# Placing accumulating transfers in the second token half, and contiguous FFN weights, in a gated-linear-attention encoder block

## The chip, the cores and the metric

The kernel runs on one core of a Trainium2 chip. The metric is the device time of one execution in microseconds (us). A core has a matrix engine (TensorE, "PE" in the profile, with its weight loads as "PEld"), a vector engine (VectorE, "DVE"), a scalar engine (ScalarE, "ACT"), a general one (GpSimd, "POOL") and SyncE ("SP"), which here only issues transfers. Each engine works through its own queue in a fixed order. DMA transfers are issued from the queues of SP, ACT and POOL; an instruction or an issue that must wait holds up everything behind it in its queue.

## The reference

One layer on 2048 tokens of width 1024, all in float32: a chunked gated linear attention mixer, then a feed-forward network with a causal convolution, each with a residual, and a final norm.

```python
h = rmsnorm(x, mix_norm_w)
x = x + gla_mixer(h, w_in, w_gate2, b_gate, norm_w, w_out)   # 4 heads, chunks of 64
h = rmsnorm(x, ffn_norm_w)
u = causal_dwconv(h @ w_up, conv_w, conv_b)   # 1024 -> 2 x 2816, 3 taps along the tokens
g, val = jnp.split(u, 2, axis=-1)
x = x + (jax.nn.silu(g) * val) @ w_down       # 2816 -> 1024
return rmsnorm(x, final_norm_w)
```

## The kernel before

**Products.** Large products are done in a fast scheme of seven instead of eight block products (`p1` to `p7`, a 2 x 2 block scheme with sums of blocks as operands). Each operand is split into a rounded part and a remainder (`split`, lines 188 and 189: a cast on ACT, a subtraction on DVE), and each block product is three matmuls per 128-wide slice (`mm3p`, lines 179 to 181).

**Stages.** The mixer's passes run to about 850 us. Then comes the up phase (`phase_u`), then the down phase. The up phase takes the tokens in two halves, `s = 0` and `s = 1`, of 1024 tokens. In each half it runs over 11 groups `g`; a group is two feature tiles `f`, each with a gate part and a value part, and 14 jobs (seven products for two tiles), each job 12 matmuls. The profile names its accumulators `ua`, `ub` (product p2) and `uc`.

**Weights of a group.** `load(sg, n)` fetches the four weight blocks of a feature tile into two raw tiles `ur`, two blocks each, one transfer per block (line 1204). `prep`, five jobs ahead, adds and subtracts blocks on POOL (`us` and `ur`: lines 1214, 1217, 1220, 1232) and splits the result on ACT and DVE into `uw_p`.

**Accumulators.** Products p1, p6, p7 and p4 of one tile go on in one accumulator. After p1 and after p6 ACT copies it out (`copied`, line 1237, named `c`), and the next product may start only then. The results go into a tile `u` with two halo columns in front (`new_u`; POOL copies them, line 1243), of which three exist. `conv` does the taps on ACT (line 1253) and DVE (line 1255), `gated` the product of gate and value (line 1262).

**Operands of the down phase.** `gated` stores the seven token operands of the down product to the scratch `ad` in DRAM. In the second half four of them are sums that POOL makes (tiles `as`, line 1284). In the first half only blocks and parts are stored (line 1267), and the sums are made in DRAM: `gather` (line 1363) issues from POOL's queue a transfer that adds one stored operand onto another. There are four per group, each needing the one before it or the stores: p7 += p5, then p5 += p4, then p6 += p5, then p3 += p6. In the program they are written in the second half, at jobs 2, 5, 10 and 13 of a group, for the same or the preceding group of the first half (the last two in the down phase):

```python
GATHER = {2: ("p7", "p5", 0), 5: ("p6", "p5", 1), 10: ("p5", "p4", 0), 13: ("p3", "p6", 1)}
```

**Order.** The framework's planner, not the program's text, sets the order on each queue: among instructions whose inputs are ready in its model, it takes the earliest written one, and an engine that is free in the model takes a later one. No edge tied the gathers to the second half.

**Change of halves.** The seven operands of the hidden state for the new half (`h_p`, line 904, four transfers each) replace those of the old half one after another, as the last group of the first half is done with them; SP issues them, as it does the weight loads and the stores to `ad`.

**Conv weights.** `vectors` loads three taps and the bias as rows, transposes them on PE and copies them into `cw` (lines 603 to 611).

Of the kernel before, what the change touches and what calls it, by code (L numbers as in the profile page):

```python
# [10 lines left out]
F32 = mybir.dt.float32  # L11
# [3 lines left out]
ALU = mybir.AluOpType  # L15

P = 128
# [8 lines left out]
def hybrid_kernel(  # L26
# [10 lines left out]
    w_out: bass.AP,  # L37
    w_up: bass.AP,
    conv_w: bass.AP,
    conv_b: bass.AP,  # L40
    w_down: bass.AP,
    out: bass.AP,
):
    nc = tc.nc
    x = x[0]
    out = out[0]
    w_in, w_gate2, gla_norm_w, w_out = w_in[0], w_gate2[0], gla_norm_w[0], w_out[0]
    w_up, conv_w, conv_b, w_down = w_up[0], conv_w[0], conv_b[0], w_down[0]

    S, D = x.shape  # L50
    F = w_down.shape[0]
# [7 lines left out]
    HK = KT // 2  # L59
    NF = F // P  # L60
# [7 lines left out]
    SB = 8  # L68
# [43 lines left out]
    def scratch(shape, name):  # L112
        return dr.tile(shape, F32, tag=name, name=name)
# [10 lines left out]
    ad = {(s, o, q): scratch([P, 512], f"ad_{s}_{o}_{q}") for s in range(NS) for o in OPS for q in range(NQ)}  # L124

    def mm_ps(name):
        return ps.tile([P, 512], F32, tag="mm", name=name, bufs=4)

    def aux_ps(name):
        return ps.tile([P, 512], F32, tag="aux", name=name, bufs=4)  # L130

    def raw_tile(shape, name):
        return wr.tile(shape, F32, tag="raw", name=name, bufs=RB)
# [17 lines left out]
    def later_do(us, fn):  # L151
        heapq.heappush(delayed, (clock["now"] + us, next(seq), fn))
# [39 lines left out]
    ident = cst.tile([P, P], F32, name="ident")  # L192
# [3 lines left out]
    cw = cst.tile([P, 4, 2 * NF], F32, name="cw")  # L196
    halo = cst.tile([P, 2 * NF, 2], F32, name="halo")
# [161 lines left out]
    rows = {}  # L359
# [9 lines left out]
    rp = {}  # L369
# [187 lines left out]
    def gates(b, t0, t1, t2):  # L557
# [27 lines left out]
        def sums(tt):  # L585
            pd = aux_ps(f"pd_{b}_{tt}")
            for i in range(2):
                nc.tensor.matmul(pd, rp["later"], L[tt][1 - i], start=(i == 0), stop=(i == 1))
            nc.scalar.activation(es[tt], pd, AF.Exp, scale=-ITAU)
            t = b * NT + tt  # L590
            nc.sync.dma_start(ed[t], es[tt])
            later_do(TB3, lambda: totals(t, es[tt]))
            if tt + 1 < NT:
                later_do(0.4 * t2, lambda: halves(tt + 1))
# [3 lines left out]
        later_do(t0 + 4.0, lambda: halves(0))  # L598
        for tt in range(NT):
            later_do(t0 + t1 + t2 * tt, lambda tt=tt: sums(tt))  # L600


    def vectors():
        rws = rp["p"].tile([P, 512], F32, tag="s2k", name="rows", bufs=SB)
        for k in range(3):
            nc.sync.dma_start(rws[:2 * NF, k * P:(k + 1) * P], conv_w[k].rearrange("(f p) -> f p", p=P))
        nc.sync.dma_start(rws[:2 * NF, 3 * P:4 * P], conv_b.rearrange("(f p) -> f p", p=P))
        pt = aux_ps("pt_c")
        for k in range(4):
            nc.tensor.transpose(pt[:, k * 2 * NF:(k + 1) * 2 * NF], rws[:2 * NF, k * P:(k + 1) * P], ident[:2 * NF, :2 * NF])  # L610
        nc.vector.tensor_copy(cw.rearrange("p a b -> p (a b)"), pt[:, :8 * NF])


    sp = {}
# [567 lines left out]
    def tiles2(ap):  # L1182

        v = ap.rearrange("p (j c k) -> p c j k", c=2, k=P)
        return v[:, 0], v[:, 1]
# [1 line left out]
    def tiles1(ap):  # L1187
        return ap.rearrange("p (j k) -> p j k", k=P)

    wuv = w_up.rearrange("(kt p) c -> p kt c", p=P)  # L1190

    def phase_u():
        raws, wops, sums, made = {}, {}, {}, {}
        jobs = [(s, g, o, f) for s in range(NS) for g in range(NQ) for o in OPS for f in (2 * g, 2 * g + 1)]
# [3 lines left out]
        def load(sg, n):  # L1198
            s, g = divmod(sg, NQ)
            for f in (2 * g, 2 * g + 1):  # L1200
                r = raw_tile([P, 2, 512], f"ur_{s}_{f}_{n}")
                for i, (c, k) in enumerate((((f, 0), (NF + f, 0)), ((NF + f, 1), (f, 1)))[n]):
                    q = nc.scalar if s == 0 and g == 0 else nc.sync
                    q.dma_start(r[:, i, :].rearrange("p (k c) -> p k c", c=P), wuv[:, HK * k:HK * (k + 1), c * P:(c + 1) * P])
                raws[f, n] = r

        def prep(k):
# [32 lines left out]
        def new_u(s, i, f):  # L1240
            c = f + i * NF
            u = pools["us"].tile([P, TS + 2], F32, tag="u", name=f"u_{s}_{c}", bufs=3)
            nc.gpsimd.tensor_copy(u[:, 0:2], halo[:, c, :])
            made["u", i, f] = u
            return tiles2(u[:, 2:2 + TS])

# [41 lines left out]
        GATHER = {2: ("p7", "p5", 0), 5: ("p6", "p5", 1), 10: ("p5", "p4", 0), 13: ("p3", "p6", 1)}  # L1288

        load(0, 0)  # L1290
        load(0, 1)
        yield
        done = 0
        bank = {}
        for k, (s, g, o, f) in enumerate(jobs):
            if s == 1 and k % GJ in GATHER:
                dst, src, back = GATHER[k % GJ]
                gather(dst, src, g - back)
            if k % GJ in (2, 7) and k // GJ + 1 < NS * NQ:
                load(k // GJ + 1, int(k % GJ == 7))  # L1300
# [21 lines left out]
            if o == "p1":  # L1322
                a = bank["a", f] = mm_ps(f"ua_{s}_{f}")
                mm3p(a, pairs)
                made["p1", f] = copied(f"c1_{s}_{f}", a)
            elif o == "p5":
                c = bank["c", f] = aux_ps(f"uc_{s}_{f}")
                mm3p(c, pairs)
            elif o == "p6":
                a = bank["a", f]  # L1330
                mm3p(a, pairs, first=False, more=True)
                made["u2", f] = copied(f"c2_{s}_{f}", a)
            elif o == "p2":
                pb = mm_ps(f"ub_{s}_{f}")
                mm3p(pb, pairs)
                ev, _ = new_u(s, 0, f)
                nc.vector.tensor_add(ev, tiles1(pb), tiles1(made.pop(("p1", f))))  # L1337
            elif o == "p7":
                a = bank["a", f]
                mm3p(a, pairs, first=False, more=True)  # L1340
                u3 = pools["us"].tile([P, 512], F32, tag="as", name=f"c3_{s}_{f}", bufs=AB)
                nc.scalar.copy(u3, a)
                ev, od = new_u(s, 1, f)
                made["ev", f] = ev
                nc.vector.tensor_add(od, tiles1(bank["c", f]), tiles1(u3))
            elif o == "p4":
                a = bank.pop(("a", f))
                mm3p(a, pairs, first=False, more=True)
                nc.scalar.copy(made.pop(("ev", f)), tiles1(a))
                conv(s, 1, f)  # L1350
            else:
                c = bank.pop(("c", f))
                mm3p(c, pairs, first=False, more=True)
                _, od = tiles2(made["u", 0, f][:, 2:2 + TS])
                nc.vector.tensor_add(od, tiles1(c), tiles1(made.pop(("u2", f))))  # L1355
                conv(s, 0, f)
                gated(s, f)


    def gather(o, src, q):  # L1360

        if 0 <= q < NQ:
            nc.gpsimd.dma_start(ad[0, o, q], ad[0, src, q], accum_op=ALU.add, max_dma_last_dim=2048)

    units = [(o, s) for o in ("p1", "p5", "p6", "p7", "p2", "p4", "p3") for s in range(NS)]
    steps = [(o, s, q) for o, s in units for q in range(NQ)]
# [94 lines left out]
    xin[1] = load_x(1, "x")  # L1461
    first_pair()
    nc.scalar.dma_start(nw2, ffn_norm_w[0].rearrange("(kt p) -> p kt", p=P))
    later_do(12.0, vectors)
    for ps_ in PS:
        for j in range(int(ps_ == "R"), NP):
            unit(ps_, j)
# [62 lines left out]
    for n, (o, s) in enumerate(units):  # L1530
# [10 lines left out]
        for q in range(NQ):  # L1541
            k = n * NQ + q
# [18 lines left out]
_INS = [  # L1561
    "x", "mix_norm_w", "ffn_norm_w", "final_norm_w",
    "gla_w_in", "gla_w_gate2", "gla_b_gate", "gla_norm_w", "gla_w_out",
    "ffn_w_up", "ffn_conv_w", "ffn_conv_b", "ffn_w_down",
]
_OUTS = [((1, 2048, 1024), "float32")]

# [22 lines left out]
```

## Time and profile before

| | us |
|---|---|
| runs: median of 3 (lowest, highest) | 2170.98 (2165.34, 2174.02) |
| the profiled execution | 2172.34 |
| its span, first to last instruction | 2170.3 |
| PE busy | 2080.6 (96%) |
| DVE busy | 1627.6 (75%) |
| ACT busy | 1105.6 (51%) |
| POOL busy | 688.3 (32%) |

Busy shares are means over stages with different limits, so the stages are read one by one. "a<-b" in a row means that the instruction writes a and reads b; numbers at the end of tile names are left out. Rows of a view of waits give the waiting engine and line, what ended the wait, the us in total, how often, and the longest. Rows of a timeline give start, duration, engine, line, operation and, in brackets, the idle time of the engine just before and what ended it. "SPq", "ACTq" and "POOLq" are the queues' own instructions, among them the issues of transfers; "to landing" is the time from a transfer's issue to its data being there.

### The profile page before, as it was taken

How to read it: one execution, taken by the hardware profiler on the slowest of the kernel's cores; microseconds unless marked ns; L12 is line 12 of the kernel's file. 1: busy time of each engine (PE TensorE's matmuls, PEld its weight loads, DVE VectorE, ACT ScalarE, POOL GpSimd, SP SyncE). 2: the span in 40 equal slices, each digit the busy share in tenths (PEclk: the TensorE clock that was granted, in tenths of full speed). 3: DMA queues.
4: the chain of work that ended last, by engine and by line, in shares of the span. 5: the costliest groups of instructions: out<-in, count | busy, mean ns of one | idle time of the engine just before them, and what ended most of it. 6: DMA issues, size and time to landing. Idle time of an engine off the chain costs nothing.

```text
span 2170.3 us, 28933 instructions
## 1 busy us (share of the span) xinstructions
PE 2080.6 (96%) x9832; PEld 1723.4 (79%) x9832; DVE 1627.6 (75%) x2168; ACT 1105.6 (51%) x2024; POOL 688.3 (32%) x606
## 2 busy tenths in 40 slices
PE   6999999989998998899999997999999999999998
PEld 5888788878887877688787786888888877888886
DVE  8756888799888664678988875988788777457564
ACT  5555755665565775454554543554445533233342
POOL 2000011111111002345446444665665444036010
PEclk9999999999999999999999999999999999999999
DMA  6646684578557899686676679342424567354453
GB/s 220 224 165 212 211 296 139 157 228 300 170 190 261 315 332 363 224 220 157 174 199 155 177 198 294 97 122 83 136 73 122 185 244 281 95 184 160 142 180 115
DMA packets 328357, 423.30 MB, mean 195 GB/s; under 512 B 24446, under 2 KB 183342, under 8 KB 328208
## 3 DMA queue, kind: packets, MB, share of 16 engines
q1 hardware_dynamic: 284336, 346.99, 48.8%
q10 hardware_dynamic: 37536, 62.93, 8.6%
q0 software_dynamic: 6336, 11.54, 3.5%
q8 instruction: 77, 1.26, 0.2%
q14 instruction: 72, 0.59, 0.1%
HBM read 278.23 MB, written 154.66 MB: 199 GB/s over the span
## 4 chain that ended last, share of the span: by engine, by line
PE 56%; DMA 14%; DVE 13%; issue 7%; POOL 4%; ACT 3%; SPq 2%; ACTq 0%; DVEq 0%; POOLq 0%
PE pd_p L180 5%; PE pd_p L181 5%; PE pd_p L179 5%; PE ua L179 4%; PE ua L181 4%; PE ua L180 4%; DVE t L1255 3%; DMA ad_p<-ad_p 3%; PE uc L179 2%; PE uc L181 2%; PE uc L180 2%; PE mp_R L179 2%; PE mp_R L181 2%; PE mp_R L180 2%; PE mp_A L181 1%
## 5 line engine op out<-in xcount | busy, mean ns | idle before, releaser
L179 PE MATMUL ua<-h_p,uw_p 128*128 128x512 f32 x704 | 278.6, 396 | 23.9 <-ACT c L1237 23.9
L1255 DVE SCALAR_TENSOR_TENSOR t<-u,cw,t 128x1024 f32<-128x1024 f32 x176 | 285.3, 1625 | 11.9 <-ACT t L1253 10.9
L180 PE MATMUL ua<-h_p,uw_p 128*128 128x512 f32 x704 | 276.4, 393 | 0.0
L181 PE MATMUL ua<-h_p,uw_p 128*128 128x512 f32 x704 | 276.3, 392 | 0.0
L180 PE MATMUL pd_p<-dw_p,da 128*128 128x512 f32 x616 | 240.3, 390 | 3.4 <-DVE da L189 3.4
L179 PE MATMUL pd_p<-dw_p,da 128*128 128x512 f32 x616 | 240.1, 390 | 0.6 <-DVE u L1337 0.6
L181 PE MATMUL pd_p<-dw_p,da 128*128 128x512 f32 x616 | 240.0, 390 | 0.0
L189 DVE TENSOR_TENSOR da<-da_p,da 128x512 fp32r<-128x512 f32 x154 | 133.7, 921 | 104.5 <-ACT da L188 104.4
L188 ACT CAST da<-da_p 128x512 fp32r<-128x512 f32 x154 | 85.3, 619 | 207.2 <-PE pd_p L181 147.2
L188 ACT CAST uw_p<-us 128x512 fp32r<-128x512 f32 x132 | 82.1, 622 | 203.9 <-POOL us L1217 124.3
L179 PEld LDWEIGHTS ua<-h_p,uw_p 128*128 128x128 f32 x704 | 133.5, 190 | 58.6 <-ACT c L1237 31.5
L189 DVE TENSOR_TENSOR uw_p<-us,uw_p 128x512 fp32r<-128x512 f32 x132 | 136.3, 1038 | 51.7 <-ACT uw_p L188 50.4
L189 DVE TENSOR_TENSOR uw_p<-ur,uw_p 128x512 fp32r<-128x512 f32 x176 | 143.2, 842 | 40.8 <-ACT uw_p L188 40.6
L181 PEld LDWEIGHTS ua<-h_p,uw_p 128*128 128x128 f32 x704 | 133.4, 190 | 28.2
L180 PEld LDWEIGHTS ua<-h_p,uw_p 128*128 128x128 f32 x704 | 133.6, 190 | 27.4
L179 PE MATMUL uc<-h_p,uw_p 128*128 128x512 f32 x352 | 138.1, 392 | 4.5 <-issue 4.5
L1253 ACT ACTIVATE t<-u,cw 128x1024 f32<-128x1024 f32 x88 | 109.7, 1247 | 60.9 <-DVE u L1355 53.0
L180 PE MATMUL uc<-h_p,uw_p 128*128 128x512 f32 x352 | 137.8, 392 | 0.7 <-DVE uw_p L189 0.7
L180 PEld LDWEIGHTS pd_p<-dw_p,da 128*128 128x128 f32 x616 | 115.7, 188 | 28.6 <-DVE da L189 4.7
L181 PE MATMUL uc<-h_p,uw_p 128*128 128x512 f32 x352 | 137.6, 391 | 0.0
L179 PEld LDWEIGHTS pd_p<-dw_p,da 128*128 128x128 f32 x616 | 115.7, 188 | 25.1 <-DVE u L1337 1.0
L181 PEld LDWEIGHTS pd_p<-dw_p,da 128*128 128x128 f32 x616 | 115.7, 188 | 23.8
(278 smaller groups left out, 5340.9 us busy)
## 6 DMA issues: line engine op xcount, KB each, us to landing
ur<-in_ffn_w_up_dram SPq DMA_DIRECT2D x168, 256.0 KB, 4.0
da_p<-ad_p SPq DMA_DIRECT2D x154, 256.0 KB, 4.0
h_p<-hd_p SPq DMA_DIRECT2D x56, 512.0 KB, 8.6
ad_p<-t SPq DMA_DIRECT2D x110, 256.0 KB, 3.2
x<-in_x_dram SPq DMA_DIRECT2D x32, 512.0 KB, 4.7
ch<-in_ffn_w_down_dram SPq DMA_DIRECT2D x61, 256.0 KB, 3.7
hr_A_p<-h1d_p SPq DMA_DIRECT2D x56, 256.0 KB, 2.9
hr_B_p<-h1d_p SPq DMA_DIRECT2D x56, 256.0 KB, 3.3
```

The costliest lines, as they stand in the source:

```text
L179: nc.tensor.matmul(ps_ap, ah, bl, start=(first and i == 0), stop=False, **kw)
L180: nc.tensor.matmul(ps_ap, al, bh, start=False, stop=False, **kw)
L181: nc.tensor.matmul(ps_ap, ah, bh, start=False, stop=(last and i == len(pairs) - 1), **kw)
L188: nc.scalar.copy(hi, src)
L189: nc.vector.tensor_sub(lo, src, f32(hi))
L1253: nc.scalar.activation(t, u[:, 2:2 + TS], AF.Identity, scale=cw[:, 2, c:c + 1], bias=cw[:, 3, c:c + 1])
L1255: nc.vector.scalar_tensor_tensor(t, u[:, k:k + TS], cw[:, k, c:c + 1], t, op0=ALU.mult, op1=ALU.add)
```

## The change

Two things. First, `new_u` keeps its last halo copy, and `gather` issues under an order-only edge to it: in POOL's queue the gather must come after that copy. The edge adds no semaphore and no wait; it binds the planner. As `gather` is written after `new_u` calls of the second half (the first of them after the last one of the first half), each gather stands behind a halo copy of the group it is written in or of the one before.

Second, the host lays out `ffn_w_up` as blocks [22 tiles, 2 raw tiles, 128 partitions, 2 blocks, 512], in the order in which the raw tiles hold them, so that one transfer of 512 KB (4 KB per partition) fills a raw tile; before, two of 256 KB in runs of 512 bytes did. It lays out the conv weights and bias as [128, 4, 44], which one transfer from ACT's queue brings straight into `cw`; `vectors` with its four loads, four transposes and a copy goes.

```diff
-    def vectors():
-        rws = rp["p"].tile([P, 512], F32, tag="s2k", name="rows", bufs=SB)
-        for k in range(3):
-            nc.sync.dma_start(rws[:2 * NF, k * P:(k + 1) * P], conv_w[k].rearrange("(f p) -> f p", p=P))
-        nc.sync.dma_start(rws[:2 * NF, 3 * P:4 * P], conv_b.rearrange("(f p) -> f p", p=P))
-        pt = aux_ps("pt_c")
-        for k in range(4):
-            nc.tensor.transpose(pt[:, k * 2 * NF:(k + 1) * 2 * NF], rws[:2 * NF, k * P:(k + 1) * P], ident[:2 * NF, :2 * NF])
-        nc.vector.tensor_copy(cw.rearrange("p a b -> p (a b)"), pt[:, :8 * NF])
...
-                for i, (c, k) in enumerate((((f, 0), (NF + f, 0)), ((NF + f, 1), (f, 1)))[n]):
-                    q = nc.scalar if s == 0 and g == 0 else nc.sync
-                    q.dma_start(r[:, i, :].rearrange("p (k c) -> p k c", c=P), wuv[:, HK * k:HK * (k + 1), c * P:(c + 1) * P])
+                (nc.scalar if s == 0 and g == 0 else nc.sync).dma_start(r, w_up[f, n])
...
-            nc.gpsimd.tensor_copy(u[:, 0:2], halo[:, c, :])
+            upool["ins"] = nc.gpsimd.tensor_copy(u[:, 0:2], halo[:, c, :])
...
+    upool = {}
+
     def gather(o, src, q):

         if 0 <= q < NQ:
-            nc.gpsimd.dma_start(ad[0, o, q], ad[0, src, q], accum_op=ALU.add, max_dma_last_dim=2048)
+            with tc.issue_after(upool["ins"].ins):
+                nc.gpsimd.dma_start(ad[0, o, q], ad[0, src, q], accum_op=ALU.add, max_dma_last_dim=2048)
...
-    later_do(12.0, vectors)
+    nc.scalar.dma_start(cw, conv_w)
...
+    up = inputs["ffn_w_up"].reshape(2, 4, 128, 2, 22, 128).transpose(4, 0, 2, 3, 1, 5).reshape(22, 2, 128, 2, 512).copy()
+    up[:, 1] = up[:, 1, :, ::-1].copy()
+    cv = _np.concatenate([inputs["ffn_conv_w"].reshape(3, 44, 128), inputs["ffn_conv_b"].reshape(1, 44, 128)])
+    laid["ffn_conv_w"] = cv.transpose(2, 0, 1)
```

More of the change, by code (lines that the diff above doesn't have):

```diff
@@ L39, in hybrid_kernel @@
     conv_w: bass.AP,
-    conv_b: bass.AP,
     w_down: bass.AP,
@@ L47, in hybrid_kernel @@
     w_in, w_gate2, gla_norm_w, w_out = w_in[0], w_gate2[0], gla_norm_w[0], w_out[0]
-    w_up, conv_w, conv_b, w_down = w_up[0], conv_w[0], conv_b[0], w_down[0]
+    w_down = w_down[0]
     S, D = x.shape
@@ L1188, in tiles1 @@
         return ap.rearrange("p (j k) -> p j k", k=P)
-    wuv = w_up.rearrange("(kt p) c -> p kt c", p=P)
     def phase_u():
@@ L1563 @@
     "gla_w_in", "gla_w_gate2", "gla_b_gate", "gla_norm_w", "gla_w_out",
-    "ffn_w_up", "ffn_conv_w", "ffn_conv_b", "ffn_w_down",
+    "ffn_w_up", "ffn_conv_w", "ffn_w_down",
 ]
@@ L1577 @@
     arrays, args = {}, []
+    laid = dict(inputs)
+    up = inputs["ffn_w_up"].reshape(2, 4, 128, 2, 22, 128).transpose(4, 0, 2, 3, 1, 5).reshape(22, 2, 128, 2, 512).copy()
+    up[:, 1] = up[:, 1, :, ::-1].copy()
+    laid["ffn_w_up"] = up
+    cv = _np.concatenate([inputs["ffn_conv_w"].reshape(3, 44, 128), inputs["ffn_conv_b"].reshape(1, 44, 128)])
+    laid["ffn_conv_w"] = cv.transpose(2, 0, 1)
     for name in _INS:
-        a = _np.ascontiguousarray(inputs[name])
+        a = _np.ascontiguousarray(laid[name])
         arrays[f"in_{name}_dram"] = a
```

## The prediction

> **What bounds the kernel now.** I read the page, then busy time by stretches, then single matmuls, then the waits of TensorE (PE) and of POOL.
>
> ```profile
> span 2170.3 us, 28933 instructions
> ```
>
> The profiled execution took 2172.34 us, 2.0 more than its span and 1.4 more than the median 2170.98. My sum is made against 2172.34.
>
> Stretches of the FFN's up phase (each engine: busy us and instructions; then granted clock, DMA share, GB/s):
>
> ```profile
> 852.00:930.00 78.00, 67.03 (x287) 54.01 (x286) 42.83 (x52) 38.76 (x71) 28.56 (x28) 0.96 0.79 261
> 930.00:1245.00 315.00, 306.20 (x1333) 248.75 (x1332) 270.50 (x276) 161.91 (x248) 161.31 (x160) 1.00 0.68 178
> 1300.00:1360.00 60.00, 47.57 (x190) 37.84 (x190) 33.73 (x36) 22.23 (x32) 29.22 (x30) 0.91 0.90 275
> 1360.00:1727.00 367.00, 367.00 (x1621) 304.07 (x1620) 310.00 (x293) 183.04 (x275) 217.98 (x152) 1.00 0.37 112
> ```
>
> From 1360 on, in the second token half, PE never pauses: 1621 matmuls in 367 us, 0.227 each. That is the floor; only time in which PE pauses can be won. One group (two feature tiles, 14 jobs of 12 matmuls) costs 168 x 0.227 = 38.1 us. The start of a group's first p2 product marks the groups. Here are those of groups 1, 9 and 10 of the first half and 1 and 10 of the second:
>
> ```profile
> 934.44 0.39 PE L179 MATMUL ub<-h_p,uw_p 128*128 128x512 f32 x1
> ...
> 1252.44 0.39 PE L179 MATMUL ub<-h_p,uw_p 128*128 128x512 f32 x1
> ...
> 1290.52 0.39 PE L179 MATMUL ub<-h_p,uw_p 128*128 128x512 f32 x1
> ...
> 1383.89 0.39 PE L179 MATMUL ub<-h_p,uw_p 128*128 128x512 f32 x1
> ...
> 1726.61 0.39 PE L179 MATMUL ub<-h_p,uw_p 128*128 128x512 f32 x1
> ```
>
> The last nine groups took (1726.61 - 1383.89) / 9 = 38.08 us each. Eight groups of the first half took 318.0, 13.4 more than 8 x 38.08. The two groups at the change of halves took 93.4, **17.2** too much. So 30.6 us lie open.
>
> Who makes PE wait (us in total, times, longest), in 930 to 1245, in 1300 to 1360 (two rows), in 852 to 930:
>
> ```profile
> PE ua L179 <- ACT c L1237: 8.8, 13, 1.7
> ```
> ```profile
> PE ua L179 <- ACT c L1237: 7.3, 1, 7.3
> PE uc L179 <- issue: 4.5, 1, 4.5
> ```
> ```profile
> PE ua L179 <- ACT c L1237: 7.9, 2, 4.8
> ```
>
> PE waits for ScalarE (ACT) to copy an accumulator out. ACT itself is late because the copy is queued behind a weight cast whose input POOL has not added up, and POOL stands at the accumulating transfers. POOL's waits in 930 to 1245:
>
> ```profile
> POOL ad_p L1363 <- DMA ad_p<-ad_p: 69.2, 17, 7.3
> POOL ad_p L1363 <- DMA ad_p<-t: 30.4, 8, 3.9
> ```
>
> That is 99.6 us, 12.5 per group: four gathers, each waiting for the stores or for the gather before it. Although they are written in the second half, they all run in the first:
>
> ```profile
> L1363 POOL DMA_DIRECT2D ad_p<-ad_p x44: 805/813/1042, 924.0 to 1349.9; - x44
> ```
> ```profile
> DMA to landing us min/median/max: 3.7/6.0/8.1
> ```
>
> The worst place, on POOL and then on ACT:
>
> ```profile
> 1280.89 0.81 POOL L1363 DMA_DIRECT2D ad_p<-ad_p  x1 [3.87 <-DMA ad_p<-t]
> ...
> 1303.38 0.81 POOL L1363 DMA_DIRECT2D ad_p<-ad_p  x1 [6.27 <-DMA ad_p<-ad_p]
> ```
> ```profile
> 1305.75 0.62 ACT L188 CAST uw_p<-us 128x512 fp32r<-128x512 f32 x1 [13.16 <-POOL us L1214]
> ```
>
> Four gathers hold POOL from 1277 to 1304, ACT waits 13.16 us, PE 7.3.
>
> **The change part by part. The edges.** Each gather now stands behind the newest halo copy (line 1243) of the second half. Nothing is removed: 44 gathers of 0.813 us remain. In the first half POOL loses its 12.5 us of waiting per group, and ACT and PE lose theirs. What remains there is VectorE (DVE): its 270.5 busy us would fit into 315 - 13.4 = 301.6, 90%, against 310 of 367, 84%, in the half that shows no pause. So some pauses may stay: I keep 2 of 13.4 (bounds 0 and 10) and book **11.4**.
>
> At the change of halves the 7.3 us go, with the slow clock after them. The 4.5 us is another matter: it fits p3's activations of the new half, which arrive late. Transfers of 1270 to 1350 (KB each, median us to landing), and SyncE's (SP) queue:
>
> ```profile
> h_p<-hd_p SPq DMA_DIRECT2D x28, 512.0 KB, 8.2
> ur<-in_ffn_w_up_dram SPq DMA_DIRECT2D x16, 256.0 KB, 11.5
> ```
> ```profile
> 1322.30 5.47 SPq L1267 DMA_DIRECT2D ad_p<-t  x7
> 1327.87 3.04 SPq L904 DMA_DIRECT2D h_p<-hd_p  x4
> ```
> ```profile
> 1336.41 3.88 SPq L904 DMA_DIRECT2D h_p<-hd_p  x4
> ```
>
> 1340.3 + 8.2 = 1348.5, just before PE resumes. Without a pause PE asks for p3 at 1290.52 + 38.08 + 2 x 2.72 = 1334.0. The stores before these loads wait for the group's convolution, which now runs 49.1 - 38.1 = 11.0 earlier; from 1336.41 - 11 = 1325.4, less about 2 for two `ur` issues fewer, the loads end their issue at 1327.3 and land at 1335.5, 1.5 late. I keep 3 of 17.2 (bounds 0 and 12: the 28 loads are 14.7 MB, all due within one group) and book **14.2**.
>
> What does the second half pay? Per group four gathers on POOL, 3.3 us, into 367 - 218 = 149 us of POOL idle in 9.6 groups, 15 per group. Their inputs were written a group earlier or more, so I expect no wait; three of the four hang on the same halo copy and may run in one burst of 3 x 0.813 = 2.4 us ahead of a sum that ACT waits for. The slack, on POOL, ACT and PE of one such group:
>
> ```profile
> 1468.84 0.18 POOL L1243 COPY u<-halo 128x2 f32<-128x2 f32 x1 [1.22 <-DVE t L1255]
> 1469.99 1.68 POOL L1217 TENSOR_TENSOR us<-us,ur 128x512 f32<-128x512 f32 x1 [0.96 <-DVE uw_p L189]
> ```
> ```profile
> 1478.03 0.56 ACT L1237 COPY c<-ua 128x512 f32<-128x512 f32 x1
> ```
> ```profile
> 1481.81 0.39 PE L179 MATMUL ua<-h_p,uw_p 128*128 128x512 f32 x1
> ```
>
> The burst falls between these two POOL rows. The copy is done at 1478.6, PE needs it at 1481.8: **3.2 us** of slack against 2.4, and 0.96 of the burst falls into idle time. Price 0; without this cover, everything beyond 3.2 us is paid 11 times. Behind the gathers wait POOL's sums for `as` and their stores on SP, then weight loads; they slip by under 1 us. The down phase first reads p1, which no gather writes; p5 comes two units (2 x 132 x 0.227 = 60 us) later, so the last chain of three gathers (18 us) is covered: 0.
>
> DVE's length matters here:
>
> ```profile
> L1255 DVE SCALAR_TENSOR_TENSOR t<-u,cw,t 128x1024 f32<-128x1024 f32 x76 | 126.4, 1664 | 1.3 <-ACT t L1253 0.6
> ```
>
> Beside a DVE that was 86% busy (270.5 of 315) no gather took over 1.042 us. The Trainium skill, "SBUF — State Buffer", section "A bandwidth-pool intuition that's wrong (but worth ruling out)", speaks against moving them under a busy DVE: a transfer issued by GpSimd that takes some 620 ns alone takes some 3100 ns beside a DVE copy, as its descriptors wait for the shared port. By that page three would take 9.3 us, 6.1 past the slack and 67 in 11 groups, and the sum would be 2210; by the row this price is 0.
>
> **The weights.** 176 loads of 256 KB, in runs of 512 bytes, become 88 of 512 KB, 4 KB per partition. Quiet landing in the second half, and a 512 KB load with such rows:
>
> ```profile
> ur<-in_ffn_w_up_dram SPq DMA_DIRECT2D x64, 256.0 KB, 3.4
> ```
> ```profile
> x<-in_x_dram SPq DMA_DIRECT2D x32, 512.0 KB, 4.7
> ```
>
> Two of the old cost up to 6.8 one after the other, one of the new 4.7. In quiet groups this is worth 0, since PE never waits. It counts where transfers queue: at the start (852 to 930), where the second group's weights come late, I book **2** of the 7.9 us (bounds 0 and 7.9); its part at the change of halves is in the 3 above.
>
> **The conv weights.** Four loads, four transposes and a copy go; one load on ACT's queue comes:
>
> ```profile
> 65.29 0.44 PE L610 MATMUL pt_c<-ident,rows 44*128 44x44 f32 x4
> ```
> ```profile
> 0.81 0.48 ACTq L1463 DMA_DIRECT2D nw<-in_ffn_norm_w_dram  x1
> ```
>
> PE gains 0.44. The new issue costs ACT about 0.48 like its neighbour, while ACT waits for x. I book **0.4** (bounds -0.5 and 1).
>
> Sum: 11.4 + 14.2 + 2 + 0.4 = 28.0; 2172.34 - 28.0 = 2144.3, on the median's scale 2143.
>
> **The rivals.** (a) *The change of halves stays bound by transfers*: `h_p` and `ur` fill the queues whoever else runs, so 12 instead of 3 of the 17.2 stay and the 2 of the start are not won: 11 more, 2154. For it speaks the DMA share of 0.90; against it, that the gathers, four per group, leave that stretch. (b) *DVE holds the first half* at 90% load: 8 more of 13.4 stay, 2151. (c) *The burst bites*: it falls ahead of a sum with no idle time before it, and other POOL work adds to it; 1.5 to 2 us per group, 11 times, 16 to 22 us: 2159 to 2165. For it: 2.4 against 3.2 is thin. (d) *Slower: a gather waits out a DVE instruction* before its descriptors are written. Place: the burst in each second-half group. Three times (1.664 + 0.813) = 7.4, less 3.2 = 4.2, 11 times 46 us: 2189. It decides from (3.2 x 11 + 28) / 33 = 1.9 us per gather on; the rows say 0.8 to 1.04. The skill's page named above gives this rule. (e) *The change doesn't do what it says*: if the planner found halo copies of the second half early, the gathers would stay early. They need one of three `u` buffers, which the first half uses to its end; or the lost time returns at a new wait. 2171.
>
> **How the numbers follow.** Forecast 0.48; (a) 0.18; (b) 0.10; (c) 0.12; (d) 0.05; (e) 0.07. A measurement here tells about 0.5%, 11 us, from no change: faster is below 2160. Faster: 0.48 + 0.18 + 0.10 + half of (c) = 0.82; same: half of (c) + (e) = 0.13; slower 0.05. Range: down to all open losses, 30.6 + 7.9 + 0.4 = 39 off, 2132, less likely than not to be reached, so 2133; up to (c)'s end, 2166.
>
> **What would show it.** Right: gathers issued only from about 1290 on; POOL without waits at line 1363; groups of 38.1 to 38.4 us in both halves; at the change of halves at most one pause of PE, at p3, for `h_p`. Wrong: gathers above 1.1 us, or groups above 38.5 in the second half with ACT waiting on `us` before a copy; or first-half groups still near 39.7 with DVE above 90%.

## The result and the profile after

The changed kernel took 2143.53 us (median; lowest 2143.12, highest 2146.53), beside 2172.11 for the kernel before on the same chip: a ratio of **0.9877, 95% interval 0.9853 to 0.9901**. Run once more beside other variants it gave 0.9890 (0.9868 to 0.9913). The forecast was 2143, the range 2133 to 2166. The profiled execution took 2143.86 us. Its page begins:

```profile
span 2142.2 us, 28669 instructions
...
PE 2078.5 (97%) x9828; PEld 1725.6 (81%) x9828; DVE 1652.3 (77%) x2167; ACT 1104.6 (52%) x2024; POOL 712.3 (33%) x606
```

The span is 28.1 us shorter than before (2170.3): PE was busy for 2080.6 us then, 2.1 more, and idle for 89.7 us instead of 63.7, 26.0 more. The stretches (us; then each engine's busy us and instructions; granted clock, DMA share, GB/s) are the start of the up phase, its steady first half, the change of halves, the second half and the down phase:

```profile
849.00:925.00 76.00, 70.42 (x309) 57.23 (x308) 45.03 (x56) 40.61 (x74) 26.47 (x28) 0.98 0.74 267
925.00:1230.00 305.00, 304.54 (x1341) 251.08 (x1340) 275.20 (x277) 162.57 (x248) 156.62 (x130) 1.00 0.49 157
1270.00:1350.00 80.00, 77.04 (x332) 62.90 (x331) 57.58 (x60) 36.53 (x55) 43.06 (x36) 0.98 0.80 261
1350.00:1694.00 344.00, 343.04 (x1512) 283.15 (x1511) 312.99 (x273) 168.94 (x253) 238.89 (x180) 1.00 0.50 132
```

The steady first half had 306.20 us of PE in 315; now PE pauses for half a microsecond in 305. The second half, which had no pause at all, now has pauses of about 1 us in 344. Next come the starts of the first p2 product of groups 1, 2, 9 and 10 of the first half and 1 and 10 of the second. The prediction shows the same rows for before, but for group 2:

```profile
924.34 0.39 PE L178 MATMUL ub<-h_p,uw_p 128*128 128x512 f32 x1
...
963.41 0.39 PE L178 MATMUL ub<-h_p,uw_p 128*128 128x512 f32 x1
...
1230.45 0.39 PE L178 MATMUL ub<-h_p,uw_p 128*128 128x512 f32 x1
...
1268.53 0.39 PE L178 MATMUL ub<-h_p,uw_p 128*128 128x512 f32 x1
...
1349.88 0.39 PE L178 MATMUL ub<-h_p,uw_p 128*128 128x512 f32 x1
...
1694.38 0.39 PE L178 MATMUL ub<-h_p,uw_p 128*128 128x512 f32 x1
```

From these marks, from PE's first row of the up phase (852.11 before, 849.08 after) and from the spans comes the account. The last column is what the prediction booked.

| stretch, us | before | after | gained | booked |
|---|---|---|---|---|
| to PE's first row of the up phase | 852.11 | 849.08 | 3.0 | 0 (0.4 for the conv weights) |
| from there to group 1 | 82.33 | 75.26 | 7.1 | 2 |
| group 1 to 9, first half | 318.00 | 306.11 | 11.9 | 11.4 |
| group 9 over the change of halves to the second half's group 1 | 131.45 | 119.43 | 12.0 | 14.2 |
| second half, group 1 to 10 | 342.72 | 344.50 | -1.8 | 0 |
| from there to the end of the span | 443.7 | 447.8 | -4.1 | 0 |
| sum | 2170.3 | 2142.2 | 28.1 | 28.0 |

**The steady first half.** POOL's waits there (930 to 1245; us in total, times, longest) no longer contain a row of the gathers' line, which led this list with 99.6 us:

```profile
POOL us L1198 <- DMA ur<-in_ffn_w_up_dram: 77.1, 8, 11.2
```

POOL now waits where it has nothing to do, once per group, for the next weights. The gathers now start at 1276.9, in the last group of the first half, where they started at 924.0 before. (The row gives shortest, median and longest in ns, and the first and the last start.)

```profile
L1350 POOL DMA_DIRECT2D ad_p<-ad_p x44: 799/935/1423, 1276.9 to 1715.5; - x44
```

**The change of halves.** PE has one longer pause left there, at 1315.75, and one of 0.93 us at 1291.38. These are the row of PE, one of ACT, and SP's queue:

```profile
1315.75 0.47 PE L178 MATMUL uc<-h_p,uw_p 128*128 128x512 f32 x1 [2.03 <-DVE u L1321]
```
```profile
1308.98 0.62 ACT L187 CAST uw_p<-ur 128x512 fp32r<-128x512 f32 x1 [3.04 <-DMA ur<-in_ffn_w_up_dram]
```
```profile
1292.72 5.72 SPq L1251 DMA_DIRECT2D ad_p<-t  x7
1298.55 2.97 SPq L892 DMA_DIRECT2D h_p<-hd_p  x4
1301.63 1.14 SPq L1188 DMA_DIRECT2D ur<-in_ffn_w_up_dram  x2
1302.87 2.73 SPq L892 DMA_DIRECT2D h_p<-hd_p  x4
```

The last of p3's four activation loads by itself, from the view of transfers:

```profile
L892 SPq DMA_DIRECT2D h_p<-hd_p x1: 610/610/610, 1305.0 to 1305.0; - x1
...
DMA to landing us min/median/max: 10.6/10.6/10.6
```

The pause is at p3, where it was forecast, and two things come right ahead of its end. The last of p3's activations, issued at 1305.0, lands 10.6 us later, at 1315.6. The sum on DVE that the row of PE names ends at the same time: the raw weights of the next group, issued at 1301.63 behind seven stores and four loads, are late too. The cast of them waits 3.04 us on ACT, the convolution's first step is queued behind it, and that step's result on DVE is queued ahead of the sum. The profile names whichever came last, here by some 0.05 us. But the product reads `h_p` and `uw_p`, not the `u` which that sum writes, and in e7, e8 and e12 a pause of 2.2, 2.4 and 2.1 us at the same product is put down to the activations. Here is the row of e7:

```profile
PE uc L178 <- DMA h_p<-hd_p: 2.2, 1, 2.2
```

So PE waits for p3's activations, and the late weights come to the same moment beside them.

**The second half.** In one of the late groups POOL stands 7.07 us for the second pair of raw weights, because SP had first issued four stores of sums that POOL was still making. The burst of gathers then comes on top, and PE pauses:

```profile
1606.31 5.44 SPq L1270 DMA_DIRECT2D ad_p<-as_p  x4
1611.84 0.89 SPq L1188 DMA_DIRECT2D ur<-in_ffn_w_up_dram  x2
```
```profile
1618.47 1.72 POOL L1198 TENSOR_TENSOR us<-ur,ur 128x512 f32<-128x512 f32 x1 [7.07 <-DMA ur<-in_ffn_w_up_dram]
...
1626.56 0.83 POOL L1350 DMA_DIRECT2D ad_p<-ad_p  x1
1627.13 1.59 POOL L1201 TENSOR_TENSOR us<-us,ur 128x512 f32<-128x512 f32 x1
1628.37 1.97 POOL L1350 DMA_DIRECT2D ad_p<-ad_p  x2
```
```profile
1639.39 0.50 PE L178 MATMUL ua<-h_p,uw_p 128*128 128x512 f32 x1 [0.80 <-ACT c L1221]
```

**The down phase.** The last group's gathers fall between POOL's subtractions for the down weights. One subtraction on DVE, 0.68 us elsewhere, takes 6.73:

```profile
1709.62 6.73 DVE L188 TENSOR_TENSOR da<-da_p,da 128x512 fp32r<-128x512 f32 x1
```
```profile
1709.08 1.68 POOL L1350 DMA_DIRECT2D ad_p<-ad_p  x2
1710.18 5.61 POOL L1407 TENSOR_TENSOR ch<-ch,ch 128x512 f32<-128x512 f32 x4
```
```profile
PE pd_p L179 <- DVE da L188: 3.9, 1, 3.9
```

A pause of 3.9 us ends at 1733.92, and then comes a stretch at a granted clock of 0.92 in which PE, though never pausing, issues 125 matmuls in 30 us instead of 134, 9 x 0.227 = 2.0 us less:

```profile
1735.03:1765.03 30.00, 30.00 (x125) 24.58 (x124) 18.19 (x21) 8.91 (x16) 8.42 (x5) 0.92 0.89 334
1765.03:1795.03 30.00, 30.00 (x134) 24.86 (x133) 21.26 (x22) 12.45 (x23) 16.42 (x11) 1.00 0.85 299
```

### The profile page after: what moved, and what is told of

Same layout as the page of the kernel before. It is cut to its first block, busy times and chain, and to the rows that moved or that the text cites. A ratio compares the mean times of both kernels' runs of the same rounds, so it can differ in the third digit from the quotient of the medians.

```text
span 2142.2 us, 28669 instructions
## 1 busy us (share of the span) xinstructions
PE 2078.5 (97%) x9828; PEld 1725.6 (81%) x9828; DVE 1652.3 (77%) x2167; ACT 1104.6 (52%) x2024; POOL 712.3 (33%) x606
## 2 busy tenths in 40 slices
DMA packets 248022, 423.27 MB, mean 198 GB/s; under 512 B 23010, under 2 KB 91746, under 8 KB 247876
## 3 DMA queue, kind: packets, MB, share of 16 engines
q1 hardware_dynamic: 207508, 346.89, 48.4%
## 4 chain that ended last, share of the span: by engine, by line
PE 58%; DVE 14%; issue 9%; DMA 8%; POOL 7%; ACT 2%; SPq 1%; ACTq 0%; DVEq 0%; POOLq 0%
PE pd_p L179 6%; PE pd_p L180 6%; PE pd_p L178 6%; DVE t L1239 4%; DVE uw_p L188 3%; PE ua L178 3%; PE ua L180 3%; PE ua L179 3%; DMA ur<-in_ffn_w_up_dram 3%; PE mp_Y L180 2%; PE mp_Y L179 2%; PE mp_Y L178 2%; DMA h_p<-hd_p 2%; POOL us L1198 2%; PE mp_B L180 2%
## 5 line engine op out<-in xcount | busy, mean ns | idle before, releaser
L1239 DVE SCALAR_TENSOR_TENSOR t<-u,cw,t 128x1024 f32<-128x1024 f32 x176 | 289.6, 1649 | 8.5 <-ACT t L1237 7.6
L188 DVE TENSOR_TENSOR da<-da_p,da 128x512 fp32r<-128x512 f32 x154 | 138.9, 955 | 104.1 <-ACT da L187 104.1
L188 DVE TENSOR_TENSOR uw_p<-us,uw_p 128x512 fp32r<-128x512 f32 x132 | 140.8, 1075 | 35.0 <-ACT uw_p L187 34.4
L178 PEld LDWEIGHTS ua<-h_p,uw_p 128*128 128x128 f32 x704 | 132.5, 188 | 39.5 <-ACT c L1221 12.2
```

Of the source, the lines that this page charges most:

```text
L178: nc.tensor.matmul(ps_ap, ah, bl, start=(first and i == 0), stop=False, **kw)
L188: nc.vector.tensor_sub(lo, src, f32(hi))
L1239: nc.vector.scalar_tensor_tensor(t, u[:, k:k + TS], cw[:, k, c:c + 1], t, op0=ALU.mult, op1=ALU.add)
```

## The experiments

The theory was that of the prediction: POOL's waits at the gathers cost the first half and the change of halves; in the second half POOL's idle time takes the gathers in; the weights matter only where transfers queue. The table gives for each kernel's profile the same stretches as above, read from the same marks. The kernel before in the first group of runs was at 2171.38, in the second at 2167.48, in the third at 2170.68 and in the fourth at 2171.47; ratios are to it.

| kernel | ratio (interval) | start | g1 to g9 | change of halves | second half | to the end |
|---|---|---|---|---|---|---|
| before | 1 | 82.3 | 318.0 | 131.5 | 342.7 | 443.7 |
| the change | 0.9877 (0.9853, 0.9901) | 75.3 | 306.1 | 119.4 | 344.5 | 447.8 |
| the change, again (e9) | 0.9890 (0.9868, 0.9913) | 75.2 | 306.0 | 118.3 | 346.4 | 447.2 |
| edges alone (e1) | 0.9901 (0.9877, 0.9925) | 80.1 | 305.1 | 121.9 | 342.7 | 444.5 |
| weights alone (e2) | 0.9985 (0.9974, 0.9995) | 75.3 | 323.5 | 131.3 | 342.7 | 442.9 |
| conv weights alone (e3) | 1.0004 (0.9990, 1.0017) | 77.0 | 320.0 | 132.5 | 342.7 | 444.1 |
| no gathers (e4) | 0.9862 (0.9842, 0.9882) | 76.2 | 306.3 | 118.4 | 342.7 | 444.6 |
| twice the gathers (e5) | 1.0064 (1.0044, 1.0084) | 75.8 | 305.7 | 125.5 | 376.7 | 443.5 |
| gathers late in the first half (e6) | 0.9909 (0.9882, 0.9936) | 75.9 | 310.6 | 122.5 | 342.7 | 444.8 |
| two transfers per raw tile (e7) | 0.9883 (0.9861, 0.9905) | 77.6 | 305.1 | 118.6 | 343.4 | 444.9 |
| half the raw weights from ACT (e8) | 0.9876 (0.9851, 0.9901) | 76.3 | 305.9 | 119.3 | 342.7 | 443.7 |
| the same, again (e12) | 0.9854 (0.9830, 0.9878) | 76.0 | 306.0 | 120.1 | 342.7 | 442.7 |
| last activations from ACT (e10) | 0.9905 (0.9885, 0.9925) | 76.0 | 306.3 | 124.9 | 343.6 | 448.5 |
| both from ACT (e11) | 0.9890 (0.9865, 0.9914) | 76.3 | 306.5 | 126.4 | 342.7 | 444.1 |

### The parts one by one (e1, e2, e3)

e1 is the kernel before with the edges and nothing else:

```diff
-            nc.gpsimd.tensor_copy(u[:, 0:2], halo[:, c, :])
+            upool["ins"] = nc.gpsimd.tensor_copy(u[:, 0:2], halo[:, c, :])
...
-            nc.gpsimd.dma_start(ad[0, o, q], ad[0, src, q], accum_op=ALU.add, max_dma_last_dim=2048)
+            with tc.issue_after(upool["ins"].ins):
+                nc.gpsimd.dma_start(ad[0, o, q], ad[0, src, q], accum_op=ALU.add, max_dma_last_dim=2048)
```

> The kernel before with the order-only edges alone; weights and conv weights as before. Theory (the edges carry the gain): the eight steady groups of the first half fall to 38.1 to 38.3 us (11.9 of 13.4 us won, as with the whole change), the change of halves gives 8 to 12 more, the start of the up phase nothing, and the down phase pays about 4: 2150 to 2156 in all. Rival (the layout carries the start and the change of halves, where transfers queue): only the 12 us of the steady groups come, less what the down phase pays: 2160 to 2165.

Measured: 2149.64 us, 0.9901. Groups 1 and 9 of the first half in its profile:

```profile
933.19 0.39 PE L179 MATMUL ub<-h_p,uw_p 128*128 128x512 f32 x1
...
1238.33 0.39 PE L179 MATMUL ub<-h_p,uw_p 128*128 128x512 f32 x1
```

Eight groups take 305.14 us, 38.14 each. The edges alone bring the whole gain of the steady first half, and 0.99% where the whole change brings 1.23 and 1.10. They leave the second half at its floor. The time lies just below the 2150 to 2156 of the theory; the down phase, for which it kept 4 us, pays only 0.8. At the change of halves the edges alone win 9.6 us, the weights alone (e2, below) 0.2, and both together 12.0 and 13.2, so the weights win some 3 us there once the gathers no longer hold POOL.

e2 has the weights in the new order, with the old gathers and the old conv weights:

```diff
-                for i, (c, k) in enumerate((((f, 0), (NF + f, 0)), ((NF + f, 1), (f, 1)))[n]):
-                    q = nc.scalar if s == 0 and g == 0 else nc.sync
-                    q.dma_start(r[:, i, :].rearrange("p (k c) -> p k c", c=P), wuv[:, HK * k:HK * (k + 1), c * P:(c + 1) * P])
+                (nc.scalar if s == 0 and g == 0 else nc.sync).dma_start(r, w_up[f, n])
```

> The kernel before with the contiguous up weights alone; gathers and conv weights as before. Theory: the steady groups keep their 39.7 us, since POOL still stands at the gathers; the start of the up phase wins its 7 us and the change of halves 0 to 3: 2162 to 2168. Rival: the transfers, not the gathers, set the change of halves, and 10 us or more come there: 2150 to 2158.

Measured: 2168.9 us, 0.9985: a gain of 0.15%, a little below what the theory said, and far from the rival's. POOL still stands at the gathers in 930 to 1245:

```profile
POOL ad_p L1359 <- DMA ad_p<-ad_p: 69.8, 15, 8.7
POOL ad_p L1359 <- DMA ad_p<-t: 30.7, 8, 3.9
```

That is 100.5 us against 99.6 before, so the weights' new order doesn't shorten the gathers' waits. In this profile the start won its 7.0 us and the change of halves 0.2, as the theory said, but the steady groups took 323.5 us, 5.5 more than before; why is not shown.

e3 brings the conv weights in by one transfer:

```diff
-    later_do(12.0, vectors)
+    nc.scalar.dma_start(cw, conv_w)
```

> The kernel before with the conv weights brought in by one transfer, nothing else. Theory: 0.4 us, not to be told from none: 2170 to 2173. Rival: the 3.0 us by which the up phase starts earlier in the changed kernel are its doing (four loads, four transposes and a copy less in a tight start): 2167 to 2169.

Measured: 2171.83 us, 1.0004: no difference. PE's first row of the up phase is at 852.41, so the 3.0 us by which the changed kernel got there earlier (849.08) are not this edit's. In other kernels' profiles that row lies between 846.4 and 855.9 without order; it is taken as scatter of the mixer.

### Without the gathers (e4)

The 44 transfers are left out, so the sums of the first half's operands are missing:

```diff
-            with tc.issue_after(upool["ins"].ins):
-                nc.gpsimd.dma_start(ad[0, o, q], ad[0, src, q], accum_op=ALU.add, max_dma_last_dim=2048)
+            pass
```

> The changed kernel without its 44 accumulating transfers: the sums in DRAM for the first half's operands are left out, everything else is as in the changed kernel. It shows what the gathers still cost where they now stand. Theory: 1.8 us in the second half and 4 at the start of the down phase, so 2137 to 2141. Rival (the burst delays the second half by more than its group times show, or contention with VectorE costs elsewhere): 2125 to 2133. Third: the price was none, and the 6 us come from somewhere else: 2142 to 2145.

Measured: 2142.02 us, 0.9862. By its time the third expectation is met, no price. By the ratios this kernel is 0.15% below the change's first run and 0.28% below its second, 3 and 6 us, with intervals that overlap. So the times allow a price of a few microseconds and don't show one. The profile shows where it would lie: the second half is at its floor, and the down phase is 3.2 us shorter than in the change's first profile.

### The wait or the load (e6)

The gathers go back beside the first half's groups, but two to three groups behind the step that makes their inputs, so that none has to wait:

```diff
-        GATHER = {2: ("p7", "p5", 0), 5: ("p6", "p5", 1), 10: ("p5", "p4", 0), 13: ("p3", "p6", 1)}
+        GATHER = {2: ("p7", "p5", 2), 5: ("p6", "p5", 3), 10: ("p5", "p4", 2), 13: ("p3", "p6", 3)}
...
-            if s == 1 and k % GJ in GATHER:
+            if k % GJ in GATHER:
...
-                gather(dst, src, g - back)
+                gather(dst, src, s * NQ + g - back)
...
```

> The changed kernel with the accumulating transfers put back into the first half, beside the groups of matmuls that they ran beside before, but held by their order two to three groups behind the step that makes their input, so that POOL never has to wait for the transfer ahead of one. It tells the wait from the load. Theory (before, the loss of the steady first half was POOL standing still in front of its next transfer; the transfers' own time is not what costs): groups of 38.1 to 38.4 us in the steady first half with the transfers in it, no row of a wait at the transfers' line, 2142 to 2150. Rival (the first half has no room for the transfers at all, because DVE and POOL are fuller there): groups of 39 us and more, 2153 and above.

The two gathers of the down phase go as well, since the last of the 44 now come at the start of the second half. Measured: 2147.59 us, 0.9909, inside the theory's bounds. Groups 2 and 10 of the first half, and group 2 of the kernel before:

```profile
971.53 0.39 PE L178 MATMUL ub<-h_p,uw_p 128*128 128x512 f32 x1
...
1280.42 0.39 PE L178 MATMUL ub<-h_p,uw_p 128*128 128x512 f32 x1
```
```profile
973.73 0.39 PE L179 MATMUL ub<-h_p,uw_p 128*128 128x512 f32 x1
```

Eight groups take 308.89 us, 38.61 each. The same eight groups took 1290.52 - 973.73 = 316.79 us, 39.60 each, before, and 1268.53 - 963.41 = 305.12, 38.14 each, with the change. POOL's waits in 930 to 1245 show 0.4 us at the gathers' line. Of the 1.46 us per group that the change won there, 0.99 were the gathers' waits and 0.47 their presence in that half. The theory holds for the larger part, some two thirds; the 38.1 to 38.4 it asked for were just missed.

### How much room the second half has (e5)

Each gather is followed by a second transfer of the same shape onto a spare tile:

```diff
+                nc.gpsimd.dma_start(scratch([P, 512], f"dump_{o}_{q}"), ad[0, src, q], accum_op=ALU.add, max_dma_last_dim=2048)
```

> The changed kernel with each of the 44 accumulating transfers followed by a second one of the same shape, from the same source onto a spare tile, so that POOL spends twice as long on them in each group of the second half. In the profile of the changed kernel three transfers with little between them took about 2.4 us of POOL, and the slack I had read before the prediction was 3.2 us. Theory (the second half has little left: the burst is hidden only because it is shorter than the slack): a doubled burst of some 4.9 us reaches past it by 1.7 us in each of 10 or 11 groups, +10 to +19, 2155 to 2163. Rival (POOL is idle for most of the second half and takes any such load): +0 to +4, at most 2147.

Measured: 2183.08 us, 1.0064, some 40 us above the change: more than either expectation. Groups 1 to 10 of the second half take 376.67 us, (376.67 - 342.72) / 9 = 3.8 us over the floor each. The last four transfers of one burst of six on POOL, the cast on ACT that waits for the sum behind it, and PE:

```profile
1446.76 1.44 POOL L1350 DMA_DIRECT2D ad_p<-ad_p  x1
1448.79 0.81 POOL L1351 DMA_DIRECT2D dump_p<-ad_p  x1 [0.59 <-issue]
1450.49 0.83 POOL L1350 DMA_DIRECT2D ad_p<-ad_p  x1 [0.90 <-issue]
1452.35 0.82 POOL L1351 DMA_DIRECT2D dump_p<-ad_p  x1 [1.02 <-issue]
```
```profile
1454.52 0.62 ACT L187 CAST uw_p<-us 128x512 fp32r<-128x512 f32 x1 [6.44 <-POOL us L1201]
```
```profile
1462.15 0.79 PE L178 MATMUL ua<-h_p,uw_p 128*128 128x512 f32 x1 [3.75 <-ACT c L1221]
```

The chain is the one drawn before the prediction: burst, sum, cast, the copy queued behind it, PE. What was wrong is the price of a longer burst: six transfers don't take 6 x 0.813 = 4.9 us. POOL pauses 0.6 to 1.0 us ahead of the later ones, for nothing that the profile shows, and four of them take 1446.76 to 1453.17, 6.4 us. The cover of the burst of three was real but thin: with twice the transfers the rival of the biting burst, (c), comes true.

### Late raw weights in the second half (e7, e8, e12)

e7 keeps the new order but loads each raw tile by two transfers of 256 KB:

```diff
-                (nc.scalar if s == 0 and g == 0 else nc.sync).dma_start(r, w_up[f, n])
+                for i in range(2):
+                    (nc.scalar if s == 0 and g == 0 else nc.sync).dma_start(r[:, i, :], w_up[f, n][:, i, :])
```

> The changed kernel with the host's contiguous layout of the up weights, but each raw tile of 512 KB loaded by two transfers of 256 KB, as many as before the change. It tells the layout from the size of one transfer. Theory (the 1.8 us that the second half lost come from a 512 KB transfer that landed late behind the four stores ahead of it; two of half the size let the first half of the tile land earlier but the tile is whole at the same time): between 2141 and 2144, the groups of the second half at 38.08 to 38.3. Rival (the gain at the start of the up phase and at the change of halves comes from fewer issues on SP's queue): 2146 to 2150.

Measured: 2143.57 us, 0.9883, as the change and as the theory said. So the number of issues on SP's queue is not what the new order brings. The second half has one group of 38.72 us and eight at the floor.

e8 moves the second pair of raw tiles of each second-half group to ACT's queue:

```diff
-                (nc.scalar if s == 0 and g == 0 else nc.sync).dma_start(r, w_up[f, n])
+                (nc.scalar if (s == 0 and g == 0) or (s == 1 and n == 1) else nc.sync).dma_start(r, w_up[f, n])
```

> The changed kernel with half of the second half's raw weight loads (the second raw tile of each group) issued by ACT instead of SP, so that they do not stand behind the four stores of the convolution state on SP's queue. Theory (the two late groups of the second half, 1.8 us together, wait for such a load): both go, 2141 to 2143. Rival (issuing from ACT takes ACT's time between two casts, and the load comes no earlier than ACT reaches it): 2144 to 2150.

Measured: 2140.93 us, just below the 2141 to 2143 of the theory, but by its ratio of 0.9876 no different from the change. In the profile the late groups are gone and the last stretch takes 443.7 us. Whether the two late groups and the long down phase were scatter of one profile was then asked of the change itself:

> The changed kernel as it is, once more, beside the two that follow, so that differences of a few us can be read and so that a second profile tells which parts of its time are scatter. In its first profile the second half was 1.8 us longer than the kernel before's (two late groups) and the down phase 4.1 us. Theory (both are scatter of that one profile: the variants' profiles had second halves of 38.08 us a group and down phases of 443.5 to 444.9 us): ten groups of 38.08 to 38.2 and a down phase of 443 to 445.5 us; 2138 to 2145. Rival (they belong to the change): two late groups and 447 us or more again.

Measured: 2147.37 us, 0.9890. The rival is right: six late groups (3.7 us together), a down phase of 447.2 us and the same subtraction of 6.73 us on DVE. The marks of the second half's groups 1 and 10, and PE's waits from 1694 to 1800:

```profile
1348.18 0.39 PE L179 MATMUL ub<-h_p,uw_p 128*128 128x512 f32 x1
...
1694.56 0.39 PE L179 MATMUL ub<-h_p,uw_p 128*128 128x512 f32 x1
```
```profile
PE pd_p L180 <- DVE da L189: 4.5, 2, 3.9
```

So e8's kernel was run once more:

> The kernel of run e8 once more, in five rounds: the changed kernel with half of the second half's raw weight loads issued by ACT. The changed kernel's two profiles both show late groups in the second half (1.8 and 3.7 us together) and a down phase of 447 us with a subtraction of 6.73 us on DVE; the profile of e8 shows neither (groups of 38.08 us, 443.7 us). Theory (both belong to the change and go with the late raw weights): 5 to 6 us below the changed kernel, whose ratios to the kernel before were 0.9877 and 0.989, so 0.985 to 0.987, with the second half at 38.08 us a group and a down phase of 443 to 445 us. Rival (what is saved there comes back elsewhere, or the profiles of e8 were lucky): 0.9875 to 0.989.

Measured: 2137.95 us, **0.9854** (0.9830 to 0.9878), as the theory said. The second half:

```profile
1350.98 0.39 PE L179 MATMUL ub<-h_p,uw_p 128*128 128x512 f32 x1
...
1693.70 0.39 PE L179 MATMUL ub<-h_p,uw_p 128*128 128x512 f32 x1
```
```profile
1609.30 1.29 POOL L1199 TENSOR_TENSOR us<-ur,ur 128x512 f32<-128x512 f32 x1 [1.40 <-DMA ur<-in_ffn_w_up_dram]
```

342.72 us, 38.08 each, and POOL, which stood 7.07 us at this place, stands 1.40. Over the second half POOL waits for raw weights 10.8 us in e8 and 11.5 here, beside 41.5 in the change and 39.7 in e4, which has no gathers and no pause either. Both profiles of this kernel have neither the late groups nor the long down phase, by the stretches 1.8 and 4 to 5 us less than the change's first profile. It is the fastest of the kernels here; its two ratios, 0.9876 and 0.9854, lie below the change's 0.9877 and 0.9890, but the intervals overlap, so the profiles show the gain and the times only point to it.

### The rest at the change of halves (e10, e11)

e10 issues the second half's activations of p2 and p3 from ACT, e11 does that on top of e8:

```diff
-            nc.sync.dma_start(f32(t[:, :, j, :]), hd[s, o, j])
+            (nc.scalar if s == 1 and o in ("p2", "p3") else nc.sync).dma_start(f32(t[:, :, j, :]), hd[s, o, j])
```

> The changed kernel with the last two operands' tiles of activations (the products p2 and p3, four loads each) of the second token half issued by ACT instead of SP, so that they do not stand behind seven stores on SP's queue, and the raw weights behind them come earlier too. Theory (the pause of the changed kernel at the change of halves is SP's queue: stores that wait, the last activations behind them and the raw weights behind those): the pause of 2.2 us of PE at p3 goes and the two spacings at the change of halves, 39.35 and 42.0, fall to 38.1 to 40, so 2 to 4 us off, a ratio to the kernel before of about 0.986. Rival (eight issues of half a microsecond each on ACT hold up the casts of the next weights by as much): no gain, 0.9875 to 0.989.

> The same as the run before it (the last two operands' activations of the second half issued by ACT), and half of the second half's raw weight loads issued by ACT too. Theory (both waits are of SP's queue and add up): 0.985 to 0.986 of the kernel before, the second half at 38.08 us a group. Rival (the raw weights from ACT bring nothing that is not scatter): the same as the run before it within 0.1%.

Measured: 2150.8 us, 0.9905, and 2147.29, 0.9890. Both theories fall: e10 is slower even than its rival said, and e11, 0.15% below e10, is far from 0.985 to 0.986. The pause at p3 goes, but the stretch gets longer, 124.9 and 126.4 us against 119.4 and 118.3. ACT's queue and ACT in e10:

```profile
1298.71 7.36 ACTq L892 DMA_DIRECT2D h_p<-hd_p  x3
1306.11 1.66 ACT L187 CAST uw_p<-ur 128x512 fp32r<-128x512 f32 x3 [6.35 <-DMA h_p<-hd_p]
```

Three issues held ACT's queue for 7.36 us, and the casts behind them waited 6.35. PE then pauses 5.5 us for a copy behind these casts, and 9.5 at the same place in e11. The same loads wait wherever they stand; on ACT the casts that feed PE stand behind them. How the two are to be had without a pause was not tried further.

## Why the prediction was right, and where it was not

The forecast (2143) came out to the microsecond (2143.53), but partly because errors cancel, and by the second run's ratio, 0.9890, the time would be 2148. Point by point, by its own steps:

- **Edges, steady first half, 11.4 booked, 11.9 came.** Right in size and reason. e1 shows the gain without the weights, e6 that the waits made up two thirds of it and the gathers' presence one third. Of the 2 us kept for DVE 1.5 stayed (306.11 - 8 x 38.08), 1.0 of them in the first group; DVE was busy for 275.20 us in 305, 90%. Rival (b) is out.
- **Change of halves, 14.2 booked, 12.0 came.** The forecast pause came where it was forecast and for the reason given: p3's activations, forecast 1.5 us late, cost a pause of 2.03 us, and e7, e8 and e12 put it down to them. The size was off: 3 of the 17.2 were kept and 5.2 stayed, as PE also paused 0.93 us at 1291.38 and had a granted clock of 0.91 from 1300 to 1320 (20 x 0.09 = 1.8 us, an estimate). In e9 the same pause, 2.04 us, is not followed by a slow clock, and its stretch is 1.1 us shorter. What the prediction did not see are the raw weights, late by as much. e8 and e12 take part of them off SP's queue, and the pause stays, 2.44 and 2.14 us. Rival (a), 12 of 17.2 staying, is out; a part of its mechanism may lie in what stayed, as the DMA share from 1300 to 1320 is 1.04, but no run took the transfers away.
- **Second half, price 0.** Nearly right in a kernel of 2143 us, but the two profiles of the change show 1.8 and 3.7 us of late groups: the burst of three fits into its slack only while the raw weights are in time. The prediction looked at the burst and the cover, not at what comes ahead of it. In these profiles it takes both: e1 (gathers here, old weights), e2 (new weights, no gathers here), e4 and e8 are at the floor. Rival (c) had the right place, and its sign, groups above 38.5 us, came in two groups of the first profile (39.19 and 38.53) and in five of the second. Its size needs more than this kernel has: at twice the transfers it costs 3.8 us a group.
- **Down phase, price 0.** This step failed: 4.1 and 3.6 us. The prediction asked only when the gathers' results are read, not what POOL and DVE do beside the last gathers. In e4, without them, the same four subtractions on POOL leave DVE at 0.68 to 1.85 us per instruction; with them one DVE instruction takes 6.73. Which one is hit depends on DVE's order. In e1, e7, e8, e11 and e12 it is a step of the convolution (7.21 to 7.25 us), the pause comes within 7 us of the phase's start (1705.03 in the change), and the last stretch takes 442.7 to 444.9 us; in both profiles of the change and in e10 it is an operand of the down product (6.70 to 6.73), the pause comes 28 to 29 us in, and the stretch takes 447.2 to 448.5. Why the later pause costs more is shown only as far as the slow clock after it, 2.0 us.
- **Start of the up phase, 2 booked, 7.1 came.** Mis-sized. The three profiles with the old order of the weights have 77.0, 80.1 and 82.3 us there, the eleven with the new order 75.2 to 77.6: on the mean about 4 us belong to the weights, though the 77.0 of e3 is no longer than some with the new order; the rest is the profile of before having been a bad one. The bounds 0 and 7.9 held it.
- **Conv weights, 0.4.** e3 can't tell it from nothing.
- **Rival (d), a gather that waits out a DVE instruction.** By the figure of the Trainium skill, "SBUF — State Buffer", section "A bandwidth-pool intuition that's wrong (but worth ruling out)", three of them would have taken 9.3 us, an estimate. The trace does not bear it out: beside a DVE 91% busy (312.99 of 344) the gathers' median is 0.935 us and their longest 1.423, where the rival needed 1.9 per gather. The figure of the Trainium skill is for a DVE copy, and the DVE work here is of other kinds. One sign of being wrong did come: 17 of the 44 gathers took over 1.1 us. They stand in the bursts, where rows overlap; two in a row, shown above, took 1.97 us together. **Rival (e)** is out by the gathers' first start, 1276.9.
- **A reading.** The prediction says that all gathers ran in the first half. The last four, from 1328.3 to 1349.9, ran in the first group of the second, inside the stretch of the change of halves.

The unforeseen gains (3.0 + 5.1 + 0.5) and the unforeseen losses (2.2 + 1.8 + 4.1, and the 0.4) are 8.6 and 8.5 us. That the sum was exact is luck; that the sign and the large terms were right is not, since each was read from a wait that the runs then took away alone.

## What to carry to other kernels

When one engine's queue holds transfers that wait for one another, ask whether the wait or the work costs: here the wait made up two thirds of the loss of the steady groups, and the work itself a third. Before booking a moved burst at nothing, look also at what else is late in its new place (a load behind stores on the same queue) and at what runs beside its last instance in the next stage. In e10 and e11 loads that had to wait for their tile stood on ACT ahead of the casts that feed PE, and cost more than they won; in e8 and e12 loads on ACT whose issue took 0.33 us each in the second half did no harm.

## What the runs showed of the hardware that was not expected

**A DVE instruction of 6.73 us.** With two gathers and four two-input subtractions back to back on POOL, one DVE instruction with two operands took 6.73 us (the change) and up to 7.25 (e8, e12). Without the gathers (e4) POOL's four subtractions took 6.90 us instead of 5.61, and DVE's subtraction beside them 1.78:

```profile
1705.04 6.90 POOL L1406 TENSOR_TENSOR ch<-ch,ch 128x512 f32<-128x512 f32 x4
```
```profile
1709.01 1.78 DVE L188 TENSOR_TENSOR dw_p<-ch,dw_p 128x512 fp32r<-128x512 f32 x1
```

That the two slow each other down agrees with the Trainium skill, "SBUF — State Buffer", section "Who interferes with whom": a DVE instruction with two inputs in SBUF contends with a GpSimd instruction that reads SBUF. In all eight profiles in which two gathers stand directly ahead of the four subtractions, POOL's four take 5.56 to 5.61 us and one DVE instruction 6.70 to 7.25. In the five in which none does (before, e2, e3, e4, e6) the four take 6.89 to 6.92, and no DVE instruction of that part of the phase takes over 2.33. So the gathers ahead of them make the difference between taking turns and one standing still for all four; why is not shown.

**Transfers of POOL in a row.** Three gathers of a burst took 0.8 to 1.0 us of POOL each (single rows, which overlap, up to 1.42); from about the fourth on (e5) POOL paused 0.6 to 1.0 us ahead of each.

**Longer runs hardly changed the transfers' time.** The page of the profile counts 328357 DMA packets before and 248022 after, but the share of time of the queue that carries the weights went from 48.8% to 48.4% only.
